# Moving the start of the backward mLSTM states from the value columns to the last key column

## The chip, the cores and the metric

The kernel runs on one core of a Trainium2 chip. The metric is device time in microseconds (us). Before the change the median of three runs is 3072.43 us, the runs reaching from 3066.46 to 3081.08.

## The reference

One encoder layer on x (2048 tokens, width 1024) and mem (256 tokens), all in float32. Two groups of channels work side by side on one combined input projection `P = rmsnorm(x) @ w_in`:

- Hyena (512 channels): a centred convolution of width 3 on v, x1, x2, then twice `z = gate * (longconv(z) + skip * z)`, where the long convolution goes over the whole length by a Fourier transform, with filters made by a small network; at the end an RMS norm per group of 64 channels.
- mLSTM (4 heads of 128 channels): convolution and SiLU on q and k, then a chunkwise matrix-state recurrence, once from the left and once from the right, each with its own gates, the two summed and gated. A state is

```
C_new = carry_decay * C + einsum('bhs,bhsd,bhse->bhde', we, k, v)
```

with a normaliser n carried likewise, and a chunk's output needs the state at its border, of both directions.

Both outputs are joined, multiplied by `w_out` and added to x; then follow cross attention into mem (whose keys and values are folded with their projections into two matrices beforehand), a squared-ReLU MLP of width 4096, and a last norm.

## The kernel before, in words

All of it is one program, written as Python generators that record instructions; each `yield` gives a weight, and `weave` takes the next step of the one of two generators that lags behind. The recorded program is then ordered by a scheduler with a timeline of its own (`schedule_with_timeline_sim=True`), which fixes the order on each engine; instructions that are recorded under `keep_in_program_order` stay in the order in which they were recorded. Each engine runs its list in order, SyncE (SP) too, whose list is nearly all loads and stores.

Large products run as three float32r products of high and low halves (lines 355, 358, 359). Tokens are worked on in two halves of 1024. The parts that matter here, in the order of the program:

- `sweep` (line 748) projects columns of `P` in transposed form, with the convolution behind it (line 845 transposes, lines 837, 849 and 858 store q, k and the natural k, called kn, to DRAM). A column yields four times. Columns 4 to 9 are mLSTM's and hyena's remaining columns; the last of the list, 8 and 9, are keys.
- `natural` (line 860) projects v and o (and the gates' columns) in their natural form (tokens on partitions); line 896 stores v to the DRAM tensor vd. A tile yields twice.
- `gates` (line 1076) turns gate columns into scales and decays, in six steps; its last step makes the columns that every state needs.
- `states` (line 1223) opens a pool `m_b` and runs `backward` over 15 chunks from the right. Per chunk there are a load of keys kn (line 1178) and of values va (line 1184) on SP, a column of ones (line 1185), a scaling of va in place on GpSimd (POOL, line 1196), four products of TensorE (line 1200, 129 columns each) that are pinned in program order, four operations on VectorE that make the new state (lines 1202, 1206), and a store of it to the DRAM tensor cbd from POOL's queue (line 1219). There are two buffers each of kn and va, so the loads of an update wait for the products of the update two before it.
- `hyena` runs woven beside all of these. Its middle part takes, for each of two orders and 16 blocks, loads of filters (fs) and spectra (zs) on SP (line 920, with constant blocks em and dm, lines 949 and 944), products (lines 956, 1030, 987), products on POOL (line 1035) and a store on POOL (line 989). Its last part (lines 974, 173 and 186, then 1051 to 1068) makes the output yh, which POOL scales and stores.
- `memproj` folds the attention's weights with mem: products L708 (projections), L725 (keys, 256 columns) and L737 (values, 512 columns); ScalarE (ACT) copies them out (line 715) and POOL's queue stores them (lines 727, 739).
- `mlstm` makes the output by 16 chunks from the left. A chunk has scores (line 1284), masks and scales on POOL, ACT and VectorE (lines 1290 to 1294), outputs (lines 1322 and 1324; the backward state comes from cbd as the tile cbn, lines 1258 and 1259), a division (lines 1327 to 1338) and the forward state's own update (again line 1200, reading the tile ve that ACT scales at line 1194). Chunk 0 needs the last backward state. The first five chunks are recorded beside the steps of `memproj`, the rest beside attention.
- The output projection loads yh and weights we (lines 1473 and 1405), split by ACT and VectorE (line 366).

The order around the change is set in `program` (line 2100 on). `among(g, h, every)` takes one step of h behind every so many steps of g and runs out what is left of h at the end.

Of the kernel before, what the change touches and what calls it, by code (L numbers as in the profile page):

```python
# [2076 lines left out]
def chain(*gens):  # L2077
    for g in gens:
        yield from g


def weave(a, b, wa, wb, until=False):
    da = db = 0.0
    fa = fb = False
    while not (fa and fb):
        if fb or (not fa and da / wa <= db / wb):
            try:
                da += next(a)
            except StopIteration:
                fa = True  # L2090
        else:
            try:
                db += next(b)
            except StopIteration:
                fb = True
                if until:
                    return


def program(p):  # L2100
    with ExitStack() as ms:
        with ExitStack() as es:
            p.inproj_open(es)
            p.filters_open()
            p.prepq = p.x_first()
            p.pop()
            s = chain(p.sweep(range(4), 0, True, lambda: p.prep_x(1)), p.opened(), p.sweep(range(4), 1, False))
            f = p.filters()
            for _ in range(5):
                next(s)  # L2110
            next(f)
            next(f)
            next(s)
            weave(s, f, 140, 102, True)
            p.gates_open(es)
            n = p.memproj()
            m = p.mlstm(ms)
            with ExitStack() as hs:
                rest = chain(s, p.sweep(range(4, 10), 1, True), p.natural(1, (3, 0, 1, 2), True),
                             p.natural(0, (3,)), among(p.sweep((4, 5, 8, 9), 0, False), p.gates(), 2),  # L2120
                             among(chain(p.natural(0, (0, 1)), p.sweep((6, 7), 0, False),
                                         p.natural(0, (2,), p.prep_mem, 2)), p.states(), 1),
                             )
                weave(rest, p.hyena(hs), 445, 329)
            for _ in chain(p.turned_in(), take(n, 1), beside_each(n, take(m, 5))):
                pass
        with ExitStack() as rs:
            p.ts = rs.enter_context(ExitStack())
            p.tail_open(p.ts)
            with ExitStack() as at:  # L2130
                g = p.attention(at)
                weave(g, m, 440, 112, True)
                ms.close()
                p.ffn_open(rs)
                for _ in g:
                    pass
            p.ffn()


def among(g, h, every):  # L2140
    for i, v in enumerate(g):
        yield v
        if i % every == every - 1:
            next(h, None)
    for _ in h:
        pass


def beside_each(g, h):
    for v in g:  # L2150
        yield v
        yield next(h, 0)
    yield from h


def take(g, n):
    for _ in range(n):
        v = next(g, None)
        if v is None:
            return  # L2160
        yield v
# [31 lines left out]
```

## Time and profile before

| | |
|---|---|
| median of 3 runs | 3072.43 us |
| the profiled execution | 3076.22 us, of which the span is 3074.5 |
| mean granted clock of TensorE | 0.987 |
| TensorE busy | 2984.5 us, 97% |
| VectorE busy | 1938.8 us, 63% |
| ACT busy | 1493.0 us, 49% |
| POOL busy | 1259.7 us, 41% |
| moved by DMA | 607.03 MB, mean 197 GB/s |
| first and last backward update (L1200 reading va) | 843.6 and 1087.2 us |
| first product of mLSTM's chunk 0 (L1322) | 1121.99 us |

Busy times are those of one profiled execution. Times like 843.6 are measured from the start of its span. In a row of the trace, `out<-in` are the program's names of the tiles, what stands in brackets is the idle time of the engine just before with what ended it, and one float32 product of TensorE shows as two records.

### The profile page before, as it was taken

The numbers are of one execution on the slowest core, as the hardware profiler recorded it, in microseconds if no ns is written. First come the engines' busy times: TensorE is split into PE (matmuls) and PEld (weight loads), VectorE is DVE, ScalarE is ACT, GpSimd is POOL, SyncE is SP. The second block draws the span as 40 slices with busy tenths as digits, with TensorE's granted clock in tenths as the row PEclk, the third lists the DMA queues.
The fourth block names the chain that finished last, engine by engine and source line by source line (L and its number), as shares of the span: only waits on it lengthen the run. The fifth ranks groups of instructions, "written<-read, shape, count | busy, mean of one in ns | idle before, by whom it ended". The sixth has DMA issues, their size and how long they took to land.

```text
span 3074.5 us, 44129 instructions
## 1 busy us (share of the span) xinstructions
PE 2984.5 (97%) x14799; PEld 2369.8 (77%) x14799; DVE 1938.8 (63%) x3442; ACT 1493.0 (49%) x2930; POOL 1259.7 (41%) x1025
## 2 busy tenths in 40 slices
PE   9999999998999988999999999999999999999998
PEld 7666667775678757888887888888888888888876
DVE  7855454657656347867665665557555676566695
ACT  6443455635654236555544455556555543333335
POOL 0112123411344654333133247765566374344653
PEclk9999999999999988999999999999999999999999
DMA  6655687596877965464567466657544565344434
GB/s 219 196 188 171 214 271 219 184 297 200 258 223 249 349 231 192 158 220 131 188 203 259 147 210 216 208 181 243 186 154 151 195 198 171 118 158 120 155 103 164
DMA packets 423643, 607.03 MB, mean 197 GB/s; under 512 B 36846, under 2 KB 229998, under 8 KB 422392
## 3 DMA queue, kind: packets, MB, share of 16 engines
q1 hardware_dynamic: 395972, 525.42, 53.3%
q0 software_dynamic: 18992, 62.96, 5.6%
q10 hardware_dynamic: 8452, 15.83, 1.4%
q8 instruction: 117, 1.92, 0.3%
q14 instruction: 110, 0.90, 0.1%
HBM read 401.67 MB, written 202.41 MB: 196 GB/s over the span
## 4 chain that ended last, share of the span: by engine, by line
PE 58%; DVE 2%; DMA 1%; issue 1%; ACT 0%; POOL 0%; SPq 0%; DVEq 0%; ACTq 0%; POOLq 0%
PE mm L355 12%; PE mm L359 12%; PE mm L358 12%; PE hy L355 6%; PE hy L359 6%; PE hy L358 6%; PE hy L1322 1%; PE hy L1324 1%; DVE bl L1693 0%; PE hy L1284 0%; PE hy L1479 0%; PE hy L1596 0%; DVE acc L1991 0%; PE hy L1200 0%; DVE acc L2028 0%
## 5 line engine op out<-in xcount | busy, mean ns | idle before, releaser
L1692 ACT CAST ah<-w 128x512 fp32r<-128x512 f32 x284 | 176.7, 623 | 304.0 <-PE hy L358 157.8
L1693 DVE TENSOR_TENSOR bl<-wr,bh 128x512 fp32r<-128x512 f32 x213 | 235.5, 1110 | 131.1 <-ACT bh L1692 131.0
L366 DVE TENSOR_TENSOR wl<-wn,wh 128x512 fp32r<-128x512 f32 (+1 forms) x296 | 216.6, 775 | 94.3 <-ACT wh L366 94.3
L355 PE MATMUL mm<-xh,wh 128*128 128x512 f32 x640 | 263.3, 413 | 3.7 <-ACT wh L366 1.2
L358 PE MATMUL mm<-xl,wh 128*128 128x512 f32 x640 | 254.1, 397 | 4.5 <-DVE xl L366 4.4
L1692 ACT CAST bh<-wr 128x512 fp32r<-128x512 f32 x232 | 143.4, 621 | 229.0 <-PE mm L359 177.5
L359 PE MATMUL mm<-xh,wl 128*128 128x512 f32 x640 | 253.7, 397 | 0.0
L1693 DVE TENSOR_TENSOR al<-w,ah 128x512 fp32r<-128x512 f32 x236 | 213.6, 905 | 55.7 <-ACT ah L1692 55.6
L359 PE MATMUL mm<-bh,al 128*128 128x512 f32 x576 | 223.7, 391 | 4.0 <-DVE al L1693 4.0
L355 PE MATMUL mm<-bh,ah 128*128 128x512 f32 x576 | 225.8, 392 | 0.1
L358 PE MATMUL mm<-bl,ah 128*128 128x512 f32 x576 | 224.9, 390 | 0.0
L366 ACT CAST wh<-wn 128x512 fp32r<-128x512 f32 (+1 forms) x296 | 164.4, 620 | 105.8 <-PE mm L359 51.0
L358 PE MATMUL mm<-act,wh 128*128 128x512 f32 x512 | 202.0, 394 | 0.0
L355 PE MATMUL mm<-act,wh 128*128 128x512 f32 x512 | 199.4, 396 | 2.0 <-ACT wh L366 1.9
L359 PE MATMUL mm<-act,wl 128*128 128x512 f32 x512 | 199.9, 392 | 0.0
L355 PE MATMUL hy<-bh,ah 128*128 128x512 f32 x448 | 175.2, 391 | 0.0
L358 PE MATMUL hy<-bl,ah 128*128 128x512 f32 x448 | 174.6, 390 | 0.0
L359 PE MATMUL hy<-bh,al 128*128 128x512 f32 x448 | 174.4, 390 | 0.0
L331 POOL TENSOR_TENSOR b<-b 128x512 f32<-128x512 f32 x32 | 48.1, 1505 | 294.6 <-DVE b L330 275.2
L355 PEld LDWEIGHTS mm<-xh,wh 128*128 128x128 f32 x640 | 120.5, 188 | 53.1 <-issue 19.4
L358 PEld LDWEIGHTS mm<-xl,wh 128*128 128x128 f32 x640 | 120.6, 188 | 49.2 <-issue 18.6
L355 PE MATMUL mm<-wh,xh 128*128 128x256 f32 (+1 forms) x512 | 154.7, 302 | 0.0
(396 smaller groups left out, 8262.9 us busy)
## 6 DMA issues: line engine op xcount, KB each, us to landing
wr<-hc SPq DMA_DIRECT2D x224, 256.0 KB
w<-in_ff_w_dram SPq DMA_DIRECT2D x172, 256.0 KB
hc<-wn SPq DMA_DIRECT2D x128, 256.0 KB
wn<-in_w_in_dram SPq DMA_DIRECT2D x100, 256.0 KB
hc<-q SPq DMA_DIRECT2D x96, 256.0 KB
fs<-a SPq DMA_DIRECT2D x32, 512.0 KB
zs<-a POOLq DMA_DIRECT2D x32, 512.0 KB, 6.0
a<-fs SPq DMA_DIRECT2D x64, 256.0 KB
```

What stands on the lines that cost most here:

```text
L331: nc.gpsimd.tensor_tensor(b, f, b, ALU.subtract)
L355: first = mm(ps, lh, rh, start=start, stop=False)
L358: mm(ps, lh, rl, start=False, stop=False)
L359: self.last = mm(ps, ll, rh, start=False, stop=stop)
L366: both = (self.nc.scalar.copy(hi, src), self.nc.vector.tensor_tensor(lo, src, hi.bitcast(F32), ALU.subtract))
L1322: nc.tensor.matmul(dst, nm[:, h], va[:, h], start=True, stop=state is None)
L1324: nc.tensor.matmul(dst, rows_[d, 1][:, h], state[:, h], start=False, stop=True)
L1692: self.nc.scalar.copy(hi, src)
L1693: eng.tensor_tensor(lo, src, hi.bitcast(F32), ALU.subtract)
```

## The change

Today `gates` takes one step behind every second of the 16 steps of the lower half's columns 4, 5, 8 and 9, six in all, and `states` begins behind the first step of the value columns (`natural` 0 and 1), with one step behind each following step; the updates that are left then stand in a row behind the last. Now a plan of 20 numbers rules both, one for each of the 16 steps of the columns and the 4 of the value columns: 0 is no step, 1 one of `gates`, 2 one of `states`. The six steps of `gates` stay where they were; `states` takes seven steps, four among the last key column and three among the value columns. The remaining steps go on behind each step of the columns 6 and 7 and of the last natural tile, as before.

```diff
-                             p.natural(0, (3,)), among(p.sweep((4, 5, 8, 9), 0, False), p.gates(), 2),
-                             among(chain(p.natural(0, (0, 1)), p.sweep((6, 7), 0, False),
-                                         p.natural(0, (2,), p.prep_mem, 2)), p.states(), 1),
+                             p.natural(0, (3,)),
+                             paced(chain(p.sweep((4, 5, 8, 9), 0, False), p.natural(0, (0, 1))),
+                                   p.gates(), back := p.states(), (0, 1) * 6 + (2,) * 6 + (2, 0)),
+                             among(chain(p.sweep((6, 7), 0, False), p.natural(0, (2,), p.prep_mem, 2)), back, 1),
...
+def paced(g, h1, h2, plan):
+    for v, n in zip(g, plan):
+        yield v
+        if n:
+            next((h1, h2)[n - 1], None)
+    yield from g
```

Every engine has the same instructions as before; their order differs from the last key column (about 787 us in the trace) to the third chunk of mLSTM (about 1160 us), and is the same behind it.

SP in the last key column, before. These are loads for hyena's blocks (fs, zs, dm, em) with stores of keys (st) and loads of input weights (wn).

```order
L920 DMA a<-fs_391 128x1x512
L849 DMA kn<-st 128x4x128 x2
L858 DMA kn<-st 16x128
L920 DMA a<-fs_391 128x1x512
L920 DMA a<-zs_2737 128x1x512 x2
L949 DMA em<-in_c_em_dram 128x256
L944 DMA dm<-in_c_dm_dram 128x256
L920 DMA a<-fs_391 128x1x512 x2
L920 DMA a<-zs_2737 128x1x512 x2
```

The same place now; the two pairs L1178, L1184 are the loads of the third and the fourth update.

```order
L849 DMA kn<-st 128x4x128
L1178 DMA kn<-kn 128x512
L1184 DMA va<-vd 128x4x128
L849 DMA kn<-st 128x4x128
L858 DMA kn<-st 16x128
L920 DMA a<-fs_391 128x1x512
L920 DMA a<-zs_2737 128x1x512 x2
L949 DMA em<-in_c_em_dram 128x256
L944 DMA dm<-in_c_dm_dram 128x256
L920 DMA a<-fs_391 128x1x512 x2
L1178 DMA kn<-kn 128x512
L1184 DMA va<-vd 128x4x128
```

The pairs, which stood behind all of these, now stand ahead of zs loads, the second of them between the fs and the zs loads of one block.

TensorE where `memproj` meets mLSTM's first chunk, before: L708 and L737 are projections and values of `memproj`, L173 and L186 hyena's last blocks, L1284 and L1322 scores and outputs of chunk 0.

```order
L1200 MATMUL hy<-va,kn 128x129 x4
L173 MATMUL hy<-a,e_2743 32x512
L186 MATMUL hy<-a,e_2743 32x512 x7
L708 MATMUL mm<-mt,wm 128x256 x3
L737 MATMUL mm<-wm,kt 128x512 x8
L708 MATMUL mm<-mt,wm 128x256 x6
L173 MATMUL hy<-a,e_2743 32x512
L186 MATMUL hy<-a,e_2743 32x512 x7
L708 MATMUL mm<-mt,wm 128x256 x10
L737 MATMUL mm<-wm,kt 128x512 x10
L1284 MATMUL hy<-qn,kk_t 128x128 x8
L737 MATMUL mm<-wm,kt 128x512 x6
```

Behind these stands chunk 0's first L1322. Now, around the same scores:

```order
L737 MATMUL mm<-wm,kt 128x512 x8
L708 MATMUL mm<-mt,wm 128x256 x7
L1284 MATMUL hy<-qn,kk_t 128x128 x8
L708 MATMUL mm<-mt,wm 128x256 x9
L737 MATMUL mm<-wm,kt 128x512
L1322 MATMUL hy<-va,rw 128x129 x5
```

And from the end of chunk 0's outputs to the first of chunk 1's:

```order
L737 MATMUL mm<-wm,kt 128x512 x7
L1200 MATMUL hy<-ve,kn 128x129 x4
L737 MATMUL mm<-wm,kt 128x512 x2
L1284 MATMUL hy<-qn,kk_t 128x128 x4
L737 MATMUL mm<-wm,kt 128x512
L1322 MATMUL hy<-va,rw 128x129
L737 MATMUL mm<-wm,kt 128x512 x2
```

No backward update is left there; the last stands where the twelfth stood, about 50 us of the trace earlier. Of the 32 L737, 17 stand ahead of chunk 0 now, and 15 among the chunks 0 and 1: the twelve of the last piece, and three ahead of chunk 1's own update.

SP at the same place, before: yh and we are loads for the output projection, the others are those of mLSTM's chunks.

```order
L1259 DMA kk_t<-kt 128x4x128
L1473 DMA wn<-yh 128x512 x2
L1259 DMA cbn<-cbd 128x516
L1184 DMA va<-vd 128x4x128
L1473 DMA wn<-yh 128x512
L1178 DMA kn<-kn 128x512
L1473 DMA wn<-yh 128x512
L1405 DMA we<-in_w_out_dram 128x2x256
```

And now:

```order
L1259 DMA kk_t<-kt 128x4x128
L1405 DMA we<-in_w_out_dram 128x2x256 x4
L1184 DMA va<-vd 128x4x128
L1259 DMA cbn<-cbd 128x516
L1178 DMA kn<-kn 128x512
L1178 DMA og<-od 128x512
```

All four loads of we have moved ahead of the next chunk's va, cbn and kn; the loads of yh have moved behind them.

## The prediction

> **What bounds the kernel now.** I read the busy shares of the page first, then stretches of the program against each other, then the order of events on the engine that is fullest.
>
> ```profile
> span 3074.5 us, 44129 instructions
> ...
> PE 2984.5 (97%) x14799; PEld 2369.8 (77%) x14799; DVE 1938.8 (63%) x3442; ACT 1493.0 (49%) x2930; POOL 1259.7 (41%) x1025
> ```
>
> TensorE (PE) is busy for 97% of the span, so a change of order gains only where PE is idle, at most the 90 us that are left over, and only those near the moved work. The windows view says which stretches those are (columns: busy us of each engine, granted PE clock, DMA share, GB/s).
>
> ```profile
> core 0: us, PE busy (x) PEld busy (x) DVE busy (x) ACT busy (x) POOL busy (x), PEclk, DMA share, GB/s
> 770.00:850.00 80.00, 77.81 (x376) 54.62 (x375) 52.00 (x80) 52.56 (x93) 32.17 (x35) 1.00 0.84 259
> 985.00:1092.00 107.00, 101.75 (x525) 80.93 (x525) 42.41 (x132) 26.76 (x61) 65.63 (x79) 0.97 1.02 344
> 1122.00:1170.00 48.00, 32.09 (x189) 29.26 (x187) 31.64 (x111) 26.20 (x107) 26.77 (x25) 0.75 0.61 198
> ```
>
> The first row holds the last key column, where the updates will begin. PE is nearly full and the DMA engines are busy for 84%. The second holds the trailing updates of today: PE nearly full, DMA engines saturated (1.02 at 344 GB/s). The third is the hand-off to the first chunks of the mLSTM output: PE is idle for 15.9 of 48 us, at a clock of 0.75. That is the stretch in which work could still be put. The timeline of PE shows its order:
>
> ```profile
> 1086.33 1.16 PE L1200 MATMUL hy<-va,kn 128*128 128x129 f32 x8 [2.94 <-POOL va L1196]
> ...
> 1115.05 1.95 PE L1284 MATMUL hy<-qn,kk_t 128*128 128x128 f32 x16
> 1116.84 5.32 PE L737 MATMUL mm<-wm,kt 128*128 128x512 f32 x12
> 1121.99 1.28 PE L1322 MATMUL hy<-va,rw 128*128 128x129 f32 x10
> ...
> 1124.44 0.39 PE L1324 MATMUL hy<-cbn,rw 128*128 128x129 f32 x2
> 1125.57 1.23 PE L1200 MATMUL hy<-ve,kn 128*128 128x129 f32 x8 [0.74 <-ACT ht L1336]
> ...
> 1135.22 0.67 PE L1322 MATMUL hy<-va,rw 128*128 128x129 f32 x2 [4.58 <-DVE den L1330]
> ...
> 1136.97 1.92 PE L1200 MATMUL hy<-ve,kn 128*128 128x129 f32 x8
> ...
> 1143.25 0.77 PE L1322 MATMUL hy<-va,rw 128*128 128x129 f32 x2 [2.27 <-issue]
> ```
>
> The first row is the last backward update (the tile name kn<-va tells it from the forward ones, which read ve). Chunk 0 begins at 1121.99, directly behind the last L737, the value products of the memory projection. From there on PE runs from one wait to the next.
>
> **The change part by part.**
>
> *The updates themselves.* The 15 updates stay 15, with the same loads, scalings and stores; they stand about three places earlier. PE is work-conserving through 787 to 1092, so eight records of L1200 per update cost the same at either place: nothing.
>
> *The wait that goes.* The last update waits 2.94 us for its values. The scaling of them on POOL tells why:
>
> ```profile
> 1085.24 1.03 POOL L1196 TENSOR_TENSOR va<-va,cols 128x516 f32<-128x516 f32 x1 [10.91 <-DMA va<-vd]
> ```
>
> POOL sat 10.91 us until that load landed, in the saturated stretch. In the changed order the last update stands where the twelfth stands now, with other products to run behind it, and the stretch carries three updates less of traffic. I take the whole 2.94 us as gained. What is late next there is the load of the last hyena blocks, which stand some 20 us earlier than now; I take no wait for it and bound it by the 2.94 us that it would replace.
>
> *The value products that move.* This is the largest term. The group of L737, with its 64 records:
>
> ```profile
> L737 PE MATMUL mm<-wm,kt 128*128 128x512 f32 x64 | 28.1, 592 | 0.0
> ```
>
> The program has 32 of these matmuls, two records each, so one costs 28.1 / 32 = 0.88 us of PE. All 32 stand ahead of chunk 0 today. In the changed order 17 do, and 15 stand among chunks 0 and 1. Chunk 0's first product therefore comes 15 x 0.88 = 13.2 us earlier, and with the wait 16.1 us: at 1105.9 in place of 1121.99. Its inputs permit that: the score products L1284 still stand ahead of it, with nine L708 and one L737 in between.
>
> Those 15 then have to be run between 1105.9 and chunk 1's forward update L1200. Walked in the new order, with today's durations: chunk 0's products 2.8 (1121.99 to 1124.8), seven L737 6.2, L1200 1.2, two L737 1.8, L1284 1.1, one 0.9, two 1.8, chunk 1's products 2.8 (as chunk 0's), three 2.6. That is 21.2 us, where today it takes 1136.97 - 1121.99 = 15.0. So chunk 1's update comes at 1127.1, 9.9 us earlier than now; 7.0 of the 13.2 us have been hidden in PE's idle time, above all the 4.58 us of the second wait. The chain beside PE has to be done by then. Its slowest part is a wait of ScalarE (ACT) for values:
>
> ```profile
> 1131.78 1.28 ACT L1194 ACTIVATE ve<-va,cols 128x129 f32<-128x129 f32 x4 [3.94 <-DMA va<-vd]
> ```
>
> Today PE's second half of chunk 1 is released 10.4 us after chunk 0's products end (1135.22 - 1124.8). The same 10.4 behind 1108.7 are 1119.1, and in the new order PE comes to it at about 1123: no wait. From chunk 2 on the order on PE is today's again, so 9.9 us are kept to the end. The most that could be kept: if chunk 2's products follow directly behind L1200 and L1284, at 1127.1 + 1.2 + 1.1 = 1129.4, it is 1143.25 - 1129.4 = 13.9 us. The least is nothing.
>
> The clock bears on this.
>
> ```profile
> 1130.00:1140.00 10.00, 4.49 (x23) 4.04 (x23) 5.62 (x18) 8.22 (x32) 5.01 (x5) 0.83 0.95 315
> 1140.00:1150.00 10.00, 4.92 (x25) 4.49 (x26) 6.58 (x22) 4.12 (x20) 1.73 (x2) 0.61 0.40 109
> 1150.00:1160.00 10.00, 7.07 (x30) 6.48 (x31) 7.87 (x31) 4.74 (x18) 7.31 (x7) 0.50 0.28 105
> ```
>
> Behind the wait of 4.58 us the granted clock falls to 0.83, 0.61 and 0.50, and the update L1200 takes 1.92 us where it took 1.23. I price chunk 1 at full clock, since the filling closes that gap, and chunk 2 as today. The Trainium skill (TensorE: Matmul & The Clock Gate, What's actually happening) states that the clock is halved after an idle window of about 3.4 us and given back after a busy one; the 4.58 us and the clocks behind them agree. By that rule the update at 1136.97 would run at full speed as well, an estimate of 1.92 - 1.23 = 0.7 us, and the sum below would be 9.1.
>
> *The loads that move on SyncE's queue (SP).* A pair of loads (L1178, L1184) needs the buffers of the update two before it, and SP issues in order. So it waits for updates today, here within 780 to 990 (us in total, times, longest):
>
> ```profile
> SPq L1178 <- PE hy L1200: 29.8, 7, 8.3
> ```
>
> In the key column five such pairs, where one stands today (at 844.68), now stand among the loads of hyena's filter products:
>
> ```profile
> 797.52 1.30 SPq L920 DMA_DIRECT2D a<-zs  x2
> ...
> 844.68 0.33 SPq L1178 DMA_DIRECT2D kn<-kn  x1
> 845.06 0.56 SPq L1184 DMA_DIRECT2D va<-vd  x1
> ```
>
> The pair of the fourth update now stands ahead of the zs loads issued at 797.52. It needs the second update, whose neighbours in the order are the first of these two rows of PE; the loads' user is the second:
>
> ```profile
> 803.77 0.40 PE L359 MATMUL mm<-xh,wl 128*128 128x512 f32 x1
> ...
> 811.93 1.02 PE L1030 MATMUL hy<-a,dm 128*128 128x512 f32 x2
> ```
>
> So these loads are issued some 7.5 us later (behind the update, at about 805), and their slack of 14 us shrinks to 7, less 3 us for four transfers of 128x512 f32 (0.26 MB each) at 344 GB/s: 4. It holds, narrowly; most of the other loads keep more. What PE waits for zs today, within 780 to 850 and within 690 to 790:
>
> ```profile
> PE hy L1030 <- DMA a<-zs: 1.0, 1, 1.0
> PE hy L1030 <- DMA a<-zs: 3.6, 1, 3.6
> ```
>
> Ends: a gain of the 1.0 us that stands, or 3.6 us at each of five updates, 18 us. I take 1.5, near the row of the same stretch. The traffic moved in is four updates of three transfers, 3.1 MB, or 9 us of a stretch in which the DMA engines are idle for 13 (16% of 80): cover exists, but little.
>
> *POOL.* The scaling L1196 and the store of a state now stand among hyena's products L1035 and stores L989 in its queue. One scaling takes 1.03 us and POOL is busy for 32.17 of 80 us there: nothing, unless its load is late, and then what is queued behind it is late with it, which is the case above. The gates' steps stay where they were.
>
> *The sum.* -2.9 - 13.2 + 6.2 + 1.5 = -8.4 us on the profiled execution's 3076.2 (its span of 3074.5 and 1.7 around it): 3067.8. That execution lies 3.8 us above the median of the runs, 3072.4, so the median forecast is **3064**. About 0.5%, or 15.4 us, is what a measurement of this kernel can tell from no change.
>
> **The rivals.**
>
> *More is kept.* The chunks beyond the first two follow at once. For it: the clock in the windows, and the "issue" wait ahead of 1143.25, which is no data dependence in the profile. Against it: the waits for VectorE and ScalarE return in every chunk until 1170. Without stalls in the key column it gives 3076.2 - 13.9 - 3.8 = 3058.5 (the 2.94 us are within the 13.9).
>
> *Nothing is kept.* The chunks start sooner but their loads do not: in the changed order four loads of the output projection (L1405), which wait for memory that hyena frees, stand ahead of the values of the next chunk on SP. Then ScalarE's wait for va moves to the same absolute time and chunk 2 begins at 1143 as now: 3072, or 3074 with the stalls. Against it: hyena also ends some 20 us earlier.
>
> *Slower: the key column stalls.* SP blocks on pairs whose update PE has not reached, and hyena's zs loads behind them come too late. At 3.6 us each for five updates it costs 18 us, and with the 9.9 gained, +8.1: 3080.5. It decides from 2 us per update on (9.9 / 5). For it: the slack of 14 us that becomes 4, and DMA engines that are busy for 84%. Against it: SP's seven waits of today, up to 8.3 us, left PE with one wait for zs of 1.0 us. The Trainium skill (DMA: Bandwidth & Descriptors, Anatomy of one DMA) says that DMA engines do not wait for semaphores, the issuing sequencer does, before dispatch; the 29.8 us of SP agree, and this is the page's word against the change.
>
> **How the numbers follow.** The forecast's case 0.50, more 0.18, nothing 0.18, slower 0.14. Its own range is 3060 to 3070 (stalls of 0 to 5 us, and 2 us of the runs' own spread, which reach from 3066 to 3081). The lower end of the whole range, 3056, is the case of more with 2.5 us of spread; the upper end, 3078, takes in nothing kept and the smaller half of the stalls, so that about 0.15 is left out. Faster by over 0.5% (under 3057) needs the case of more and some luck: 0.11. Slower by over 0.5% (over 3088) needs stalls beyond the 18 us: 0.06. Within: 0.83.
>
> **What would show it.** Right: chunk 0's first L1322 some 15 us earlier relative to the start of the key column, L737 among chunks 0 and 1, no wait of 4.58 us there, chunk 2's first L1322 8 to 10 us earlier, and under 3 us of PE waits between 787 and 850. Wrong: PE waits for zs or em there of over 10 us, the last update still waiting for POOL, or L1322 of chunk 2 at the same place as now.

## The result, and the profile after

The changed kernel takes 3062.82 us (median of 18 runs, 3053.97 to 3067.08), the kernel before 3073.85 (median of 18 runs, 3066.46 to 3082.51). The ratio is 0.9962 [0.9955, 0.9970], which is -11.7 us [-13.8, -9.2]. Forecast was 3064, 8.4 us under the 3072.43 that the kernel before had shown until then.

The profiled execution of the changed kernel takes 3063.97 us. From its page:

```profile
span 3062.3 us, 44144 instructions
...
PE 2979.0 (97%) x14799; PEld 2367.6 (77%) x14799; DVE 1953.2 (64%) x3442; ACT 1491.5 (49%) x2930; POOL 1263.4 (41%) x1025
```

The span is 12.2 us shorter, of which 5.5 us are PE's busy time (the mean granted clock is 0.989 in place of 0.987) and the rest idle time. The three stretches of the prediction, in the windows view (busy us of each engine, granted PE clock, DMA share, GB/s):

```profile
core 0: us, PE busy (x) PEld busy (x) DVE busy (x) ACT busy (x) POOL busy (x), PEclk, DMA share, GB/s
770.00:850.00 80.00, 77.09 (x356) 52.56 (x354) 56.79 (x98) 51.72 (x91) 34.23 (x37) 1.00 0.89 284
985.00:1092.00 107.00, 104.64 (x588) 83.76 (x573) 49.40 (x144) 27.61 (x63) 69.33 (x84) 0.98 1.02 348
1122.00:1170.00 48.00, 31.89 (x185) 27.06 (x184) 29.67 (x110) 28.42 (x110) 25.78 (x25) 0.80 0.64 202
```

At these times (the changed trace runs 4.6 us late there, as shown below) the key column's stretch is dearer (PE is busy for 0.7 us less, VectorE for 4.8 us more, the DMA engines for 89% in place of 84%), the saturated stretch is better filled, and the windows of the hand-off cannot be compared at fixed times, since the hand-off has moved. So I place the gain by three marks, read from the group view by line: the first transpose at the start of the last key column (L1171), the first output product of chunk 0 (L1322) and the first transpose of the output projection (L1479). The columns are the durations in ns, then the first and the last start in us. Before:

```profile
L1171 PE MATMUL hy<-ident,G x1: 271/271/271, 766.8 to 766.8; 128*128 128x128 f32 x1
...
L1322 PE MATMUL hy<-va,rw x256: 271/275/582, 1122.0 to 1502.8; 128*128 128x129 f32 x128
...
L1479 PE MATMUL hy<-ident,wn x128: 270/273/476, 1167.6 to 1638.4; 128*128 128x128 f32 x128
```

After:

```profile
L1171 PE MATMUL hy<-ident,G x1: 271/271/271, 771.4 to 771.4; 128*128 128x128 f32 x1
...
L1322 PE MATMUL hy<-va,rw x256: 271/275/583, 1110.6 to 1493.9; 128*128 128x129 f32 x128
...
L1479 PE MATMUL hy<-ident,wn x128: 270/273/476, 1159.4 to 1629.2; 128*128 128x128 f32 x128
```

Up to the first mark the two programs are the same, and yet the changed one gets there 4.6 us later; over all runs below this mark lies anywhere from 766.8 to 774.2, so that is chance. From the first mark to the second it needs 339.2 us where it needed 355.2 (-16.0), from the second to the third 48.8 where it needed 45.6 (+3.2). Together -12.8. Behind the third mark PE's order is the same in both, and the changed execution is 4.0 us shorter there; I put that down to chance as well, and it pays most of the 4.6 back. The gain lies where the prediction put it: chunk 0 starts earlier, and the hand-off gives a part of that back.

PE's timeline at the hand-off, after:

```profile
1104.10 1.95 PE L1284 MATMUL hy<-qn,kk_t 128*128 128x128 f32 x16
...
1109.77 1.02 PE L737 MATMUL mm<-wm,kt 128*128 128x512 f32 x2
1110.63 1.28 PE L1322 MATMUL hy<-va,rw 128*128 128x129 f32 x10
...
1113.31 6.17 PE L737 MATMUL mm<-wm,kt 128*128 128x512 f32 x14
1119.32 1.06 PE L1200 MATMUL hy<-ve,kn 128*128 128x129 f32 x8
1120.21 1.88 PE L737 MATMUL mm<-wm,kt 128*128 128x512 f32 x4
...
1128.97 2.74 PE L737 MATMUL mm<-wm,kt 128*128 128x512 f32 x6
1131.54 1.06 PE L1200 MATMUL hy<-ve,kn 128*128 128x129 f32 x8
1134.20 1.13 PE L1284 MATMUL hy<-qn,kk_t 128*128 128x128 f32 x8 [1.60 <-issue]
1135.17 0.39 PE L1322 MATMUL hy<-va,rw 128*128 128x129 f32 x2
...
1142.23 0.77 PE L1322 MATMUL hy<-va,rw 128*128 128x129 f32 x2 [5.12 <-DVE bry L213]
```

From 1110.63 to 1131.54 PE has no wait: the value products L737 fill what were waits of 0.74 and 4.58 us. In the middle of chunk 2 the wait for VectorE's L213, which was 2.81 us (at 1149.84 before), is 5.12 us now. The granted clock there:

```profile
1130.00:1140.00 10.00, 5.52 (x36) 4.20 (x35) 3.66 (x16) 6.95 (x29) 7.22 (x7) 1.00 0.90 286
1140.00:1150.00 10.00, 4.84 (x19) 4.27 (x20) 8.69 (x36) 2.60 (x11) 4.98 (x6) 0.51 0.47 161
```

It is still 1.00 to 1140, with a gap of 1.60 us and the start of the long one in the window, and 0.51 in the ten us in which the 5.12 us end.

### The profile page after: what moved, and what is told of

Read it like the earlier page. It is cut to its first block, busy times and chain, and to the rows that moved or that the text cites. A ratio compares the mean times of both kernels' runs of the same rounds, so it can differ in the third digit from the quotient of the medians.

```text
span 3062.3 us, 44144 instructions
## 1 busy us (share of the span) xinstructions
PE 2979.0 (97%) x14799; PEld 2367.6 (77%) x14799; DVE 1953.2 (64%) x3442; ACT 1491.5 (49%) x2930; POOL 1263.4 (41%) x1025
## 3 DMA queue, kind: packets, MB, share of 16 engines
q8 instruction: 117, 1.92, 0.3%
## 4 chain that ended last, share of the span: by engine, by line
PE 58%; DVE 2%; DMA 1%; issue 1%; ACT 1%; POOL 0%; SPq 0%; DVEq 0%; POOLq 0%; ACTq 0%
PE mm L355 12%; PE mm L359 12%; PE mm L358 12%; PE hy L355 6%; PE hy L359 6%; PE hy L358 6%; PE hy L1322 1%; PE hy L1324 1%; DVE bl L1693 0%; PE hy L1284 0%; PE hy L1596 0%; DVE acc L1991 0%; PE hy L1200 0%; PE hy L1479 0%; DVE acc L2028 0%
```

## The experiments

The theory of the prediction was that the gain is the *filling*: value products, which stood ahead of chunk 0, run in PE's idle time among chunks 0 and 1. The first rival was that the filling does not matter, and the gain comes from what ends earlier when the updates end earlier (loads, buffers, the list of another engine); I call it *clearing*. The second was that it is the *early start* in the key column as such. One table holds all runs; "ahead" is the number of the 32 L737 that stand ahead of chunk 0, the stages are those between the three marks, in us of the profiled execution, and the ratio is against the kernel before on the same chip. The ratio comes from all runs of a kernel, the stages from one execution: of two executions of the same kernel the first stage differs by 1.6 to 5.4 us, the second by 0.9 at most, so that the ratio decides.

| kernel | ahead | key column to chunk 0 | chunk 0 to projection | sum | ratio |
|---|---|---|---|---|---|
| before | 32 | 355.2 | 45.6 | 400.8 | 1 |
| after | 17 | 339.2 | 48.8 | 388.0 | 0.9962 [0.9955, 0.9970] |
| after_b | 17 | 340.8 | 48.7 | 389.5 | 0.9965 [0.9952, 0.9978] |
| all_first | 30 | 356.2 | 41.5 | 397.7 | 0.9985 [0.9976, 0.9994] |
| all_first_b | 30 | 350.8 | 41.5 | 392.4 | 0.9978 [0.9969, 0.9987] |
| shift1 | 16 | 336.0 | 49.2 | 385.1 | 0.9951 [0.9939, 0.9964] |
| shift1_b | 16 | 340.3 | 48.7 | 389.0 | 0.9961 [0.9947, 0.9975] |
| shift2 | 16 | 338.1 | 47.5 | 385.6 | 0.9958 [0.9946, 0.9970] |
| shift1_first | 32 | 349.0 | 39.7 | 388.7 | 0.9963 [0.9949, 0.9977] |
| shift1_first_b | 32 | 352.4 | 38.9 | 391.3 | 0.9976 [0.9965, 0.9986] |
| late_dense | 12 | 339.0 | 51.9 | 390.9 | 0.9961 [0.9947, 0.9975] |
| late_one | 19 | 342.6 | 47.9 | 390.5 | 0.9982 [0.9973, 0.9991] |
| dense_all | 0 | 318.9 | 78.6 | 397.5 | 0.9973 [0.9964, 0.9983] |
| b_pool2 | 32 | 354.2 | 41.4 | 395.6 | 0.9984 [0.9974, 0.9994] |

**Without the filling: all_first.** The changed kernel, but `memproj` is recorded to its end ahead of the chunks.

```diff
-            for _ in chain(p.turned_in(), take(n, 1), beside_each(n, take(m, 5))):
+            for _ in chain(p.turned_in(), n, take(m, 5)):
```

> The changed kernel, but with memproj's steps recorded ahead of mLSTM's first five instead of beside them; in the order 30 of the 32 value products L737 then stand ahead of chunk 0's first output product (17 in the changed kernel, 32 before). The updates stand as early as in the changed kernel. Filling (the gain is value products run in the idle time of mLSTM's first chunks): nearly all of the gain is gone, only the wait of 2.9 us and two products are left, ratio to before 0.998 to 0.999 (3068 to 3071 us beside 3074). Clearing (the gain is that updates and their traffic have left the saturated stretch in front of mLSTM): as the changed kernel, 0.996 (3062).

3066.70 us, -4.6 us by the ratio where the changed kernel has -11.7; again, as all_first_b:

> Once more the changed kernel with memproj's steps recorded ahead of mLSTM's first five (30 of 32 value products ahead of chunk 0). The theory is now of two parts: with the last updates out of the way, hyena's last blocks, their stores and the loads behind them come earlier, so that the first chunks wait less even with nothing to fill them; and the value products fill what idle time is left, for some 5 us of the 12. Two parts: 0.9975 to 0.9985. Filling alone: 0.999. No filling at all, so that the earlier run of this kernel was chance: 0.9965.

3066.89 us, -6.8 us. The first run is what filling alone had forecast, the second what the two parts had. The intervals of the first and the changed kernel do not touch; those of the second and of after_b overlap. Filling is worth about 4 to 7 us (0.9985 and 0.9978 against 0.9962 and 0.9965, of 3072); taking both runs of each kernel together, resampling the recorded times gives 5.3 us [2.7, 7.9]. The other 5 us or so are there without it. So neither theory has it alone.

**Later, and without the key column: shift1, shift2.** The plan of the 20 steps is changed alone: the updates begin at the end of the key column, one or two steps ahead of the value columns.

```diff
-  p.gates(), back := p.states(), (0, 1) * 6 + (2,) * 6 + (2, 0)),
+  p.gates(), back := p.states(), (0, 1) * 6 + (0, 0, 0) + (2,) * 5),      # shift1
+  p.gates(), back := p.states(), (0, 1) * 6 + (0, 0) + (2,) * 6),         # shift2
```

> Only one step earlier than before (the changed kernel: three): the states begin behind the last step of the last key column. The order has 16 value products ahead of chunk 0, as many as the changed kernel; one update of two products still stands behind them in the memory projection. Filling: the changed kernel's gain, 0.996 to 0.997 (3062 to 3065). Clearing: a third of it, as one update of three has left the stretch, 0.9985 to 0.999 (3069 to 3071).

> Two steps earlier: the states begin behind the last but one step of the last key column. 16 value products stand ahead of chunk 0. Filling: between the two others or as one of them, 0.995 to 0.996, the wait for VectorE in the key column between 0 and 2 us. Clearing: two thirds of the changed kernel's gain, 0.9975.

3055.84 us (-15.0) and 3062.95 us (-12.9). To see whether shift1 is better than the changed kernel, both ran again side by side:

> One step earlier, once more. Filling, with the key column's cost on VectorE: 2 to 4 us faster than the changed kernel on the same chip (ratio to before 0.995), since its first update alone lies among the keys and no wait for L960 of over 1 us arises. If the two differ only by chance: the same ratio as the changed kernel within 0.001.

> The changed kernel once more, unaltered, for a comparison on one chip with the three beside it. 0.996, with TensorE waiting for VectorE (L960) for about 1.8 us in the key column, as in its first profile, if that wait belongs to the order, and without it if it was chance.

3062.81 us (-12.0) and 3062.63 us (-10.8). The lead of shift1 did not come back. No version here is told apart from the changed kernel as faster. What they show is that most of the early start is not needed. The group view of the backward updates says how far apart the starts are. The changed kernel, then shift1:

```profile
L1200 PE MATMUL hy<-va,kn x120: 271/274/276, 791.9 to 1046.1; 128*128 128x129 f32 x120
```

```profile
L1200 PE MATMUL hy<-va,kn x120: 271/274/276, 819.4 to 1070.7; 128*128 128x129 f32 x120
```

The updates begin 27.5 us later and end 24.6 us later (31.4 and 28.5 when each is counted from its own first mark), and the kernel takes no longer.

**No update in the key column: late_dense and late_one.** The updates begin with the value columns, as before the change, and are made up for by two steps of `states` behind each of the first three steps of what follows (late_dense), or behind the first alone (late_one).

```diff
-  p.gates(), back := p.states(), (0, 1) * 6 + (2,) * 6 + (2, 0)),
-  among(chain(p.sweep((6, 7), 0, False), p.natural(0, (2,), p.prep_mem, 2)), back, 1),
+  p.gates(), back := p.states(), (0, 1) * 6 + (0,) * 4 + (2,) * 4),
+  dense(chain(p.sweep((6, 7), 0, False), p.natural(0, (2,), p.prep_mem, 2)), back, (2, 2, 2, 1, 1, 1, 1, 1, 1, 1)),
...
+def dense(g, h, plan):
+    for v, n in zip(g, plan):
+        yield v
+        for _ in range(n):
+            next(h, None)
+    for _ in h:
+        pass
```

> No update among the key columns: the states begin behind the first value step as before, but take two steps behind each of the first three steps of columns 6 and 7, so that the last update stands where the changed kernel has it. 12 value products stand ahead of chunk 0, 20 behind. Filling: at least the changed kernel's gain, 0.995 to 0.996 (3059 to 3062), since 20 products and some projections lie in the chunks. Early start (what matters is that the updates begin among the keys, away from the value columns): little or nothing, 0.999 to 1.001.

3059.54 us (-12.0). So the early start is not needed for the gain: late_dense's updates begin at 850.2, 77 us behind its first mark (773.2), as they do in the kernel before (843.6 and 766.8), and the gain is whole. They end early, though, at 1051.5:

```profile
L1200 PE MATMUL hy<-va,kn x120: 271/273/276, 850.2 to 1051.5; 128*128 128x129 f32 x120
```

Doubling them has a price in the stretch ahead of chunk 0. PE's waits there (860 to 1092), of late_dense and then of shift1:

```profile
PE hy L173 <- DMA a<-zg: 8.3, 2, 4.9
PE mm L725 <- DMA wm<-in_xa_wq_t_dram: 3.8, 1, 3.8
```

```profile
PE mm L725 <- ACT kt L710: 2.5, 1, 2.5
PE hy L173 <- DMA a<-zg: 0.7, 1, 0.7
```

Hyena's last loads and the weights of the memory projection come late, 12.1 us in all, of which shift1 has 0.7. With 12 of the value products ahead of chunk 0 in place of 16, and some of the projections L708 behind it too, late_dense seems to win a part of that back.

> The states begin where they began before the change, with no update among the keys, and take two steps once, behind the first step of column 6; all in all one update earlier than before. 19 of 32 value products stand ahead of chunk 0. Two parts: as the kernel one step earlier, 0.995 to 0.9965, with no wait for VectorE's L960 in the key column and without the waits for loads of 3 to 5 us that the doubled updates brought. If an update among the keys has a worth of its own: 0.998 or more.

3066.86 us (-5.5), 0.9982 [0.9973, 0.9991]. That is not the 0.995 to 0.9965 of the two parts; it is the 0.998 or more that was expected if an update among the keys has a worth of its own. Late_dense speaks against such a worth, since it has the gain without an update there, but these two runs alone do not settle it. Its profile has a wait of 5.7 us for the keys' copy in the saturated stretch:

```profile
PE mm L725 <- ACT kt L710: 5.7, 1, 5.7
```

The same wait is 2.4 and 4.1 us in the two profiles of the changed kernel, and 2.5 and 4.6 in the two of shift1, so that some 2 us of it can be chance. Against late_dense this kernel lacks 6.5 us by the ratio, while the sum of its stages is 0.4 us shorter. Why it lacks the rest is open, and so is whether an early update is worth something in this place.

**All updates doubled: dense_all.** The plan of the change, and two steps behind each of the first five that follow (`dense` as above).

```diff
-  among(chain(p.sweep((6, 7), 0, False), p.natural(0, (2,), p.prep_mem, 2)), back, 1),
+  dense(chain(p.sweep((6, 7), 0, False), p.natural(0, (2,), p.prep_mem, 2)), back, (2, 2, 2, 2, 2, 1, 1, 1, 1, 1)),
```

> Starts among the keys as the changed kernel, and takes two steps behind each of the first five steps of columns 6 and 7, so that no update is left behind them. No value product stands ahead of chunk 0, and keys' and projections' products lie among chunks 0 to 4 too. Filling: the idle time that the changed kernel leaves behind chunk 1 (waits of 5.1, 5.0 and 2.5 us on TensorE up to 1170) is filled as well, 0.992 to 0.995 (3050 to 3059). Clearing: as the changed kernel, 0.996. A third way: the doubled updates saturate the DMA engines in columns 6 and 7, TensorE waits there, and it is slower than the changed kernel, 0.997 to 1.000.

3060.91 us (0.9973, -8.3). No value product stands ahead of chunk 0 any more, chunk 0 comes 20 us earlier than in the changed kernel, and the hand-off is full, as one window of it shows:

```profile
1140.00:1150.00 10.00, 10.00 (x68) 8.96 (x67) 6.15 (x22) 5.39 (x24) 5.45 (x5) 1.00 0.45 128
```

And yet the sum of the stages is 9.5 us longer than the changed kernel's. PE's waits in 860 to 1092 say what was paid:

```profile
PE hy L173 <- DMA a<-zg: 8.8, 3, 5.1
PE mm L725 <- DMA wm<-in_xa_wq_t_dram: 4.6, 1, 4.6
...
PE mm L708 <- DMA wm<-in_xa_wk_dram: 0.8, 1, 0.8
```

14.2 us of waits for loads, none of which the changed kernel has in that stretch. So the filling has a limit on its other side: bringing so many updates forward makes loads behind them late. It is not that the DMA engines are fuller. Where most of the waits fall they are less busy than in the changed kernel (dense_all, then the changed kernel):

```profile
950.00:1050.00 100.00, 90.91 (x556) 73.79 (x555) 51.46 (x139) 33.31 (x68) 51.74 (x60) 0.97 0.92 291
```

```profile
950.00:1050.00 100.00, 97.64 (x595) 83.30 (x601) 49.40 (x131) 33.29 (x66) 52.80 (x63) 0.98 0.98 318
```

The loads are issued late. Hyena's last store of zg starts 195 us behind the first mark in dense_all and 183 in the changed kernel, and the first load of zg follows at 199 and 187. SP, which issues these loads in order, also waits longer for the buffers of the updates (860 to 1092, dense_all, then the changed kernel):

```profile
SPq L1178 <- PE hy L1200: 35.3, 7, 11.6
```

```profile
SPq L1178 <- PE hy L1200: 22.5, 5, 8.3
```

In late_dense this wait is 38.8 us, in shift1 25.1. Waits of this kind are what the prediction's rival "slower" rests on, here in a later stretch; how much of the 14.2 us they make was not tried.

**Shift1 without the filling: shift1_first.** The edits of shift1 and of all_first together; all 32 products stand ahead of chunk 0.

> One step earlier, but with memproj's steps recorded ahead of mLSTM's first five: all 32 value products stand ahead of chunk 0, as before the change, while the updates stand as in the kernel beside it. Filling: the gain of that kernel is gone but for the wait for the values and what its clearer stretch gives, 0.998 to 1.000. Clearing or an effect of the updates' places as such: 0.995, as the kernel beside it.

> Once more one step earlier with all 32 value products ahead of chunk 0. Two parts: 0.997 to 0.998, some 5 us slower than the same kernel without that order (0.9956 in the mean of two). Filling alone: 0.999. No filling: 0.9956.

3064.57 us (-11.4) and 3065.86 us (-7.4), against shift1's -15.0 and -12.0: filling is worth about 4 us here (4.0 [1.2, 6.8], worked out as above; run by run the intervals overlap). Filling alone had forecast 0.998 to 1.000, and both ratios lie below: with the value products where they stood before, 7 to 11 us remain.

**What else was in the way: b_pool2.** In both kernels without the filling the stage from chunk 0 on is shorter than before (41.5 and 39 us against 45.6). It holds the same products in shift1_first, and two L737 more in all_first. ACT's list shows a difference there. Before, ACT waits for chunk 2's values in the middle of chunk 1 (the row of L1194 at 1131.78, with 3.94 us of wait, stands in the prediction; here is what stands around it):

```profile
1126.56 1.28 ACT L1293 ACTIVATE rw<-rw,cols 128x128 f32<-128x128 f32 x4 [0.28 <-POOL rw L1291]
...
1132.97 0.15 ACT L1327 ACTIVATE hy<-hy 128x2 f32<-128x2 f32 x1
1133.02 1.27 ACT L1293 ACTIVATE rw<-rw,cols 128x128 f32<-128x128 f32 x4
```

L1327 and the second four L1293 belong to chunk 1, but stand behind the scaling in ACT's list and begin only when it is through. VectorE waits for them, and PE's 4.58 us end with VectorE's L1330, the operation behind this one:

```profile
1134.39 0.69 DVE L1294 TENSOR_TENSOR rw<-rw,hy 128x512 f32<-128x512 f32 x1 [2.89 <-ACT hy L1327]
```

In all_first ACT waits for the load nearly as long, but the scaling stands behind all eight L1293:

```profile
1129.90 2.71 ACT L1293 ACTIVATE rw<-rw,cols 128x128 f32<-128x128 f32 x8
1135.89 1.28 ACT L1194 ACTIVATE ve<-va,cols 128x129 f32<-128x129 f32 x4 [3.29 <-DMA va<-vd]
```

PE's wait in the middle of chunk 1 is gone there. But ACT's L1336 stands behind the scaling as well, and PE waits for that at chunk 1's update:

```profile
1140.70 2.09 PE L1200 MATMUL hy<-ve,kn 128*128 128x129 f32 x8 [5.10 <-ACT ht L1336]
```

To try ACT's list alone, b_pool2 is the kernel before with one edit: chunk 2's scaling runs on POOL.

```diff
-                update(new, cf, kk, va, 4 * n, nc.scalar)
+                update(new, cf, kk, va, 4 * n, nc.gpsimd if n == 2 else nc.scalar)
```

> The kernel before the change, with one of 16 forward scalings (chunk 2's, line 1194) moved from ScalarE to POOL (line 1196). TensorE's order is the same down to the output projection. That scaling waits for the values of chunk 2 (3.94 us in the profile before) with chunk 1's exponentials and absolute values queued behind it on ScalarE. If this queue makes TensorE's wait of 4.58 us in chunk 1: that wait goes, and the kernel is 2 to 5 us faster than before, 0.9985 to 0.9995. If the wait for the values holds chunk 2 anyway: chunk 2 begins at 1143 as before, 1.000.

3069.72 us, 0.9984 [0.9974, 0.9994], -4.9 us. Its PE timeline, then POOL's:

```profile
1091.97 1.06 PE L1200 MATMUL hy<-va,kn 128*128 128x129 f32 x8
...
1135.72 0.46 PE L1322 MATMUL hy<-va,rw 128*128 128x129 f32 x2 [1.59 <-DVE den L1330]
```

```profile
1135.78 1.05 POOL L1196 TENSOR_TENSOR ve<-va,cols 128x516 f32<-128x516 f32 x1 [2.55 <-DMA va<-vd]
```

The load still lands late, and POOL waits 2.55 us for it, but chunk 1's work on ACT no longer stands behind it: PE's wait falls from 4.58 to 1.59 us and the stage from 45.6 to 41.4. This is clearing in one instruction: the load was not too late for its own user, but for what stood behind its user in ACT's list.

It is not what shortens the stage in all_first, although that stage is as long (41.5). From chunk 0's first product to chunk 1's update it takes 15.0 us before and 11.8 in b_pool2, but 16.0 and 16.8 in all_first (with 1.8 for the two L737); from that update to the projection it takes 30.6 before and 29.5 in b_pool2, but 25.5 and 24.8 in all_first. So b_pool2 gains mostly ahead of the update, all_first behind it, and shift1_first in both parts (13.3 and 12.0, then 26.5 and 26.9). What shortens the second part, no run here isolates.

In the changed kernel the wait is gone and so is the queue behind it. The two rows of SP, before and after, show that the load itself is not issued earlier relative to chunk 0 (1126.38 is 4.4 us behind its first product, 1114.76 is 4.1):

```profile
1126.38 0.52 SPq L1184 DMA_DIRECT2D va<-vd  x1
```

```profile
1114.76 0.53 SPq L1184 DMA_DIRECT2D va<-vd  x1
```

But its scaling on ACT stands at 1122.77, behind both groups of L1293 and 8 us after the issue, while PE runs value products, and has no wait: the filling covers the load.

## Why the prediction was right, point by point

- **The time**: 3062.82 lies 1.2 us from the forecast of 3064, and a part of that is luck. The change is worth 11.7 us where 8.4 were forecast, and the kernel before took 1.4 us more in these runs than the 3072.43 that the forecast started from.
- **The updates cost nothing more on PE by moving**: so. L1200 of the backward updates takes 271 to 276 ns a record after, 271 to 378 before.
- **The wait of 2.94 us that goes**: it is gone, but the term was not one of the change. b_pool2, whose order there is that of the kernel before, runs the last update at 1091.97 without a wait. As far as these two profiles tell, the wait belongs to the one execution, so the median of the kernel before holds it only in part, and the change cannot have taken all of it from there. No load of the last hyena blocks took its place in the changed kernel.
- **15 value products behind chunk 0, -13.2**: right in place and size. With the 2.94 and the 1.5 of the key column, -14.6 was forecast for the start of chunk 0 relative to the key column; it is -16.0. The 1.4 beyond it are within what the saturated stretch gives or takes by chance.
- **Running them costs +6.2**: the term that was mis-sized; it measured +3.2. The walk of the first two chunks was right: 21.2 us were forecast from chunk 0's first product to chunk 1's update, 20.9 were measured. The step that failed is "from chunk 2 on as today": from that update to chunk 2's first product it takes 3.6 us (1131.54 to 1135.17) where it took 6.3 (1136.97 to 1143.25). The waits in between are 1.6 us in place of 3.2, and the update takes 1.06 in place of 1.92, as the clock stays at 1.00 to 1140. I had said that the filling closes the gap ahead of chunk 1 and yet priced chunk 2 at the clock which that gap had caused. The Trainium skill (TensorE: Matmul & The Clock Gate, What's actually happening) has the clock halved after an idle window of about 3.4 us. The windows of 1130 to 1150 agree (1.00 with gaps up to 1.60 us, 0.51 behind 5.12); b_pool2 is less simple, as the last section shows. By that rule the sum should have stood at the 9.1 us that I gave beside it, or more.
- **The key column, +1.5**: too much, and of another cause. PE's waits from 780 to 860 add up to 2.3 us before, 2.9 in the changed kernel and 2.3 in after_b. The wait of 1.0 us for zs is gone from there; PE waits for VectorE:

```profile
PE mm L355 <- DVE a L960: 1.8, 1, 1.8
```

VectorE has no break from 812.56 to the copy on which PE waits, and the operation that makes the new state (L1206) stands twice ahead of it:

```profile
819.04 0.60 DVE L1206 SCALAR_TENSOR_TENSOR cb<-cb,cols,hy 128x129 f32<-128x129 f32 x2
...
821.37 0.60 DVE L1206 SCALAR_TENSOR_TENSOR cb<-cb,cols,hy 128x129 f32<-128x129 f32 x2
...
825.37 0.69 DVE L960 COPY a<-mm 64x512 f32<-64x512 f32 x1
```

The two rows make 1.2 us; the order of the operations beside them has changed as well. The prediction costed the updates on PE, SP and POOL, and left out their four operations on VectorE. This wait is in all five profiles of kernels with the change's plan (the changed kernel, after_b, dense_all, all_first and all_first_b, 1.8 to 2.4 us), and in none of before, shift1, shift2 and late_dense.
- **The rival "slower"**: it did not happen. SP blocks a little longer within 780 to 990 (33.1 us where it was 29.8), with the same longest wait, and no load behind it was late:

```profile
SPq L1178 <- PE hy L1200: 33.1, 8, 8.3
```

- **The rival "nothing is kept"**: its step, that ACT's wait for chunk 2's values moves to the same absolute time, fell: that scaling stands at 1122.77 without a wait. The rival looked at the right wait, though, and so did the prediction, but for the wrong reason: both took it for a link of a chain from load to update, and the cost was in what stood behind it on ACT.
- **The rival "more is kept"**: the outcome lies between the forecast and it. In the profiles -12.8 us of the stages stand against -8.4 forecast and -13.9 of that rival.
- **Of what the gain is made**: the prediction put 7.0 us (13.2 - 6.2) on the filling, and nothing but the 2.94 on anything else. The runs put 4 to 7 us on the filling, and about 5 us on the rest. b_pool2 shows one thing that was in the way, ACT's list, worth 4.9 us in the kernel before, and the changed kernel is rid of it. That this makes the rest in the kernels without the filling is not shown: all_first gains behind chunk 1's update, where b_pool2 gains little, and shift1_first on both sides of it. What else is in the rest stays open; a kernel without the filling in which that scaling alone is put back between the two groups of L1293 was not tried.

## What to carry to other kernels

Work without a deadline that stands ahead of a chain of waits gains when it is recorded among the links of that chain: it hides their waits and keeps the clock up, as long as what is brought forward to make that possible does not make later loads late (14.2 us of waits in dense_all). Of a wait for a load, read what is queued behind the waiting instruction on its engine, before its own user: moving one scaling to another engine was worth over a third of the change (4.9 of 11.7 us). And of a step that is moved, cost every engine it touches; the one left out was the one that made PE wait.

## What the runs showed of the hardware that was not expected

- With the same order of instructions, profiled executions differ by several us in where the time goes: the first mark lies from 766.8 to 774.2 us, the wait for the keys' copy in the saturated stretch (DMA share 1.02) is 2.4 or 4.1 us in the changed kernel, and the last update waits 2.94 us or not at all in the order of before. A term of 3 us read from one profile of such a stretch is no property of the kernel.
- The granted clock stays at 1.00 in ten us in which PE is busy for only 5.52, and falls to 0.51 in the ten behind, in which one gap of 5.12 us ends. A gap of that length is not needed, though. In b_pool2 the clock is 1.00 from 1130 to 1137, with gaps of 1.59 and 0.88 us close together at 1134 to 1138, and then it is at a half:

```profile
1138.00:1147.00 9.00, 7.19 (x32) 6.74 (x32) 7.06 (x15) 7.55 (x28) 5.84 (x5) 0.50 0.63 198
```

One gap of 1.60 us in the changed kernel left it at 1.00. So neither the length of one gap nor the idle share of ten us tells by itself when it falls.
